# Single-core channel attention on Trainium2: K^T Q copied out of its PSUM banks, V cast moved to ScalarE, steps of one unit reordered

## The chip, the cores and the metric

The kernel runs on one core of a Trainium2 chip. The metric is device time in microseconds (us) of one execution. Engines are abbreviated as in the profile: PE is TensorE (PEld its weight loads), DVE is VectorE, ACT is ScalarE, POOL is GpSimd, SP starts the transfers. "Pitch" below is the time from the start of one unit's gram matmuls to the next unit's. TensorE is called "warm" when a gram takes about 1.07 us and "cold" when it takes about 1.90: in the kernel before, the granted clock was 1.00 at a gram of 1.07 us (at 161.74 us) and 0.50 at one of 1.90 us (at 81.00 us).

## The reference

For 8 x 12 heads with Q, K, V of 512 x 64 fp32:

```python
Q_norm = Q / (norm(Q, axis=-2) + 1e-10)          # columns of length 512 normalised
K_norm = K / (norm(K, axis=-2) + 1e-10)
attn = einsum('bhnd,bhne->bhde', Q_norm, K_norm)  # 64 x 64 per head
attn = softmax(attn, axis=-1)
return einsum('bhnd,bhde->bhne', V, attn)
```

## The kernel before

A unit is four heads; there are U = 24. Q and K of a unit are cast side by side into one bf16 tile `qkb`, and 64 small matmuls form its gram matrix: Q^T Q and K^T K give the norms (their diagonals), K^T Q the logits. The logits are K^T Q, scaled by 1/|k| (`kqs`), transposed by matmuls (`lgdup`), scaled by 1/|q| (`sl`), then exp, sum, normalise (`ab`). `ab` is doubled onto the other 64 partitions by a matmul. V is cast, transposed (`vps`, `vt`) and multiplied (`po`, `so`).

```python
def grams(u):
    g = gbuf[:, :, u % 2]                 # a tile in PSUM, two slots per head in use
    ...  nc.tensor.matmul(g[:, h], x, x, start=(t == 0), stop=(t == R - 1), ...)

def scale_k(u):                           # K^T Q times 1/|k|, read from the gram tile
    nc.vector.tensor_tensor(out=kk[D:], in0=gbuf[D:, :, u % 2, 0:D], in1=rq[u]..., op=ALU.mult)
...
for s in range(U + 3):                    # program order of one step
    on(load_qk, s + 3); on(load_v, s + 1); on(store, s - 6)
    on(casts, s + 1)                      # VectorE: Q and K
    on(scale_k, s - 1)                    # VectorE
    on(normalise, s - 2)                  # VectorE
    on(grams, s)                          # TensorE
    on(norms, s)                          # VectorE, then GpSimd for 1/norm
    on(vtrans, s - 2); on(outs, s - 3)    # TensorE, ScalarE copies
    on(logits, s - 1); on(scale_q, s - 1) # TensorE, VectorE
    on(cast_v, s - 1)                     # VectorE
    on(doubled, s - 2)                    # TensorE, ScalarE copy
    on(exps, s - 1)                       # ScalarE
```

In the trace each engine takes its instructions in this order (the steady unit in the prediction shows it). "Gram banks" below means the PSUM tile `gbuf`; the bank that logits and doubled attention share is the PSUM tile `lgdup`.

## Time and profile before

| | before |
|---|---|
| time, median of 3 runs | 180.92 us |
| profiled span | 177.2 us |
| gram of unit 3 / of unit 23 starts at | 24.97 / 161.74 us |
| pitch in the steady stretch | 6.83 us |

From the page of the kernel before: the busy time of each engine with its share of the span, then, over 40 slices of 4.4 us each, the TensorE clock in tenths and the bytes moved.

```profile
PE 104.3 (59%) x2712; PEld 84.9 (48%) x2712; DVE 110.2 (62%) x384; ACT 68.0 (38%) x121; POOL 29.0 (16%) x35
...
PEclk9999999686786786876876876867867867869995
...
GB/s 215 382 421 411 410 403 409 411 409 413 378 378 340 258 352 312 276 363 285 279 362 268 287 388 252 295 355 265 322 230 142 102 235 122 0 122 122 118 184 175
```

No engine is full, the clock is down to six to eight tenths from the eighth slice to near the end, and transfers slacken from about 410 to some 300 GB/s from the eleventh slice on: I read all three as engines waiting for each other. Which waits, the prediction shows.

### The profile page before, as it was taken

How to read it: one execution, taken by the hardware profiler on the slowest of the kernel's cores; microseconds unless marked ns; L12 is line 12 of the kernel's file. 1: busy time of each engine (PE TensorE's matmuls, PEld its weight loads, DVE VectorE, ACT ScalarE, POOL GpSimd, SP SyncE). 2: the span in 40 equal slices, each digit the busy share in tenths (PEclk: the TensorE clock that was granted, in tenths of full speed). 3: DMA queues.
4: the chain of work that ended last, by engine and by line, in shares of the span. 5: the costliest groups of instructions: out<-in, count | busy, mean ns of one | idle time of the engine just before them, and what ended most of it. 6: DMA issues, size and time to landing. Idle time of an engine off the chain costs nothing.

```text
span 177.2 us, 6265 instructions
## 1 busy us (share of the span) xinstructions
PE 104.3 (59%) x2712; PEld 84.9 (48%) x2712; DVE 110.2 (62%) x384; ACT 68.0 (38%) x121; POOL 29.0 (16%) x35
## 2 busy tenths in 40 slices
PE   0414847648559468477486485495594584677640
PEld 0314745537437346356365365274373473465430
DVE  0477585764765866857757757757758658567720
ACT  2000215154162361450541642632623614606981
POOL 5035202012022021120120220220220210201300
PEclk9999999686786786876876876867867867869995
DMA  5999999999999889898898898898865273033244
GB/s 215 382 421 411 410 403 409 411 409 413 378 378 340 258 352 312 276 363 285 279 362 268 287 388 252 295 355 265 322 230 142 102 235 122 0 122 122 118 184 175
DMA packets 13850, 50.72 MB, mean 286 GB/s; under 512 B 1536, under 2 KB 1536, under 8 KB 13824
## 3 DMA queue, kind: packets, MB, share of 16 engines
q1 hardware_dynamic: 13824, 50.34, 77.3%
q8 instruction: 21, 0.34, 0.8%
q14 instruction: 5, 0.04, 0.1%
HBM read 37.75 MB, written 12.58 MB: 284 GB/s over the span
## 4 chain that ended last, share of the span: by engine, by line
PE 51%; DVE 32%; DMA 4%; issue 3%; ACT 3%; POOL 2%; SPq 1%; ACTq 0%; POOLq 0%
PE gram L88 24%; PE vps L139 12%; PE lgdup L111 8%; PE po L151 8%; DVE vb L80 7%; DVE qkb L76 7%; DVE qkb L75 7%; DVE kqs L105 6%; DVE sl L115 5%; DMA kf<-in_K_dram 4%; POOL rq L100 2%; ACT so L155 2%; DVE scr L95 1%; ACT ab L133 1%; ACT ex L119 0%
## 5 line engine op out<-in xcount | busy, mean ns | idle before, releaser
L88 PE MATMUL gram<-qkb 32*128 32x128 bf16 x1536 | 44.4, 302 | 54.0 <-DVE kqs L105 47.9
L88 PEld LDWEIGHTS <-qkb 32*128 32x128 bf16 x1536 | 40.1, 137 | 69.4 <-issue 61.2
L141 ACT COPY vt<-vps 128x1024 bf16<-128x1024 bf16 x24 | 24.3, 1012 | 86.6 <-PE vps L139 86.4
L100 POOL TENSOR_TENSOR rq<-nsq,mhalf 128x4 f32<-128x4 f32 x24 | 26.6, 1107 | 136.0 <-DVE nsq L95 136.0
L95 DVE CUSTOM_DVE_ANT_0 scr<-gram,ident 128x128 f32<-128x128 f32 x96 | 22.2, 287 | 20.6 <-PE gram L88 20.6
L115 DVE TENSOR_TENSOR sl<-lgdup,rq 64x256 f32<-64x256 f32 x24 | 10.0, 417 | 28.0 <-PE lgdup L111 27.8
L155 ACT COPY so<-po 128x512 f32<-128x512 f32 x48 | 26.0, 598 | 0.5 <-PE po L151 0.5
L139 PE MATMUL vps<-identb,vb 128*128 128x128 bf16 x192 | 23.6, 298 | 0.7 <-DVE vb L80 0.7
L139 PEld LDWEIGHTS <-vb 128*128 128x128 bf16 x192 | 17.5, 134 | 6.7 <-issue 4.1
L75 DVE CAST qkb<-qf 128x1024 bf16<-128x1024 f32 x24 | 16.3, 680 | 5.5 <-DMA qf<-in_Q_dram 5.5
L151 PE MATMUL po<-ab,vt 128*32 128x128 bf16 x768 | 17.1, 239 | 1.1 <-ACT ab L133 1.1
L111 PE MATMUL lgdup<-ident,kqs 64*64 64x64 f32 x192 | 17.4, 235 | 0.0
L76 DVE CAST qkb<-kf 128x1024 bf16<-128x1024 f32 x24 | 16.3, 680 | 1.5 <-DMA kf<-in_K_dram 1.5
L80 DVE CAST vb<-vf 128x1024 bf16<-128x1024 f32 x24 | 16.2, 675 | 0.0
L151 PEld LDWEIGHTS <-vt 128*32 128x32 bf16 x768 | 12.9, 107 | 6.1 <-issue 5.0
L119 ACT ACTIVATE ex<-sl 64x256 f32<-64x256 f32 x24 | 10.0, 417 | 14.5 <-DVE sl L115 14.0
L111 PEld LDWEIGHTS lgdup<-ident,kqs 64*64 64x64 f32 x192 | 14.0, 144 | 2.9 <-issue 0.8
L132 PE MATMUL lgdup<-ab,identb 64*64 64x256 bf16 x24 | 6.6, 275 | 12.3 <-DVE sl L115 11.7
L123 DVE TENSOR_REDUCE esum<-ex 64x4 f32<-64x256 f32 x24 | 9.9, 411 | 1.8 <-ACT ex L119 1.2
L105 DVE TENSOR_TENSOR kqs<-gram,rq 64x256 f32<-64x256 f32 x24 | 10.3, 428 | 0.9
L127 DVE TENSOR_TENSOR ab<-ex,rinv 64x256 bf16<-64x256 f32 x24 | 10.0, 417 | 0.8
L133 ACT CAST ab<-lgdup 64x256 bf16<-64x256 f32 x24 | 8.8, 367 | 2.9 <-PE lgdup L132 2.3
(13 smaller groups left out, 18.5 us busy)
## 6 DMA issues: line engine op xcount, KB each, us to landing
qf<-in_Q_dram SPq DMA_DIRECT2D x24, 512.0 KB, 7.3
kf<-in_K_dram SPq DMA_DIRECT2D x24, 512.0 KB, 8.1
vf<-in_V_dram SPq DMA_DIRECT2D x24, 512.0 KB, 4.5
out_dram<-so SPq DMA_DIRECT2D x24, 512.0 KB, 5.0
```

What stands on the lines that cost most here:

```text
L75: nc.vector.tensor_copy(t_[:, :, 0:D], qf[u])
L76: nc.vector.tensor_copy(t_[:, :, D:], kf[u])
L80: nc.vector.tensor_copy(w.rearrange("p t d -> p (t d)"), vf[u])
L88: nc.tensor.matmul(g[:, h], x, x, start=(t == 0), stop=(t == R - 1), tile_position=(NV * h, 0))
L95: nc.vector.tensor_tensor_reduce(out=scr, in0=gbuf[:, h, u % 2], in1=ident, scale=1.0, scalar=1e-20, op0=ALU.mult, op1=ALU.add, accum_out= ...
L100: nc.gpsimd.tensor_tensor(out=r, in0=n2, in1=mhalf, op=ALU.pow)
L105: nc.vector.tensor_tensor(out=kk[D:], in0=gbuf[D:, :, u % 2, 0:D], in1=rq[u][D:, :, None].to_broadcast([D, HU, D]), op=ALU.mult,)
L111: nc.tensor.matmul(lg[:, h, :], kqs[u][D:, h, :], ident[D:, D:], tile_position=(D, 0))
L139: nc.tensor.transpose(ps[:, t, :], vb[u][:, t, :], identb)
L141: nc.scalar.copy(w, ps)
L151: nc.tensor.matmul(po[rows, k, :], vt[u][:, TP // 2 * i + k, rows], a[:, h].rearrange("p a d -> p (a d)"), tile_position=(0, NV * h),)
L155: nc.scalar.copy(s[:, TP // 2 * i:TP // 2 * (i + 1), :], po)
```

## The change

Its intent: take the reading of the gram banks off the slow path. ScalarE copies K^T Q out right behind the grams, unscaled, so that only that copy and the norms hold them; VectorE scales the copy later, from SBUF. The V cast goes to ScalarE, and exp, normalising and the doubling are moved to other places in the step. Cut to its core:

```diff
-    V_AHEAD = LOAD_AHEAD - 2
+    V_AHEAD = LOAD_AHEAD - 3
     def cast_v(u):
-        nc.vector.tensor_copy(w..., vf[u])
+        nc.scalar.copy(w..., vf[u])
+    def keep_kq(u):
+        nc.scalar.copy(kq[u][D:], gbuf[D:, :, 0:D])
     def scale_k(u):
-            in0=gbuf[D:, :, u % 2, 0:D], ...
+            in0=kq[u][D:], ...
@@ one step @@
+        on(exps, s - 2)
+        on(cast_v, s - 2)
+        on(cast_q, s + 1)
+        on(normalise, s - 2)
         on(scale_k, s - 1)
         on(grams, s)
+        on(keep_kq, s)
         on(norms, s)
+        on(cast_k, s + 1)
+        outs(s - 3, s - 2)     # output halves; doubling of s - 2 between the two copies
         on(logits, s - 1)
         on(scale_q, s - 1)
+        on(vtrans, s - 2)
```

The first V is also no longer loaded in front of the loop, and the gram buffer has one slot per head.

More of the change, by code (lines that the diff above doesn't have):

```diff
@@ L53 @@
     LOAD_AHEAD = 3
-    V_AHEAD = LOAD_AHEAD - 2
-    CAST_AHEAD = 1
+    V_AHEAD = LOAD_AHEAD - 3
     STORE_LAG = 6
-    qf, kf, vf, vb, qkb, nsq, rq, kqs, sl, ex, vt, so = ({} for _ in range(12))
+    qf, kf, vf, vb, qkb, nsq, rq, kqs, sl, ex, vt, so, kq = ({} for _ in range(13))
     def load_qk(u):
@@ L71, in store, with cast_q, cast_k @@
         nc.sync.dma_start(out=Of[u], in_=so[u].rearrange("p t d -> p (t d)"))
-    def casts(u):
-        t_ = qkb[u] = qkp.tile([128, R, 2 * D], BF16, name="qkb")
-        nc.vector.tensor_copy(t_[:, :, 0:D], qf[u])
-        nc.vector.tensor_copy(t_[:, :, D:], kf[u])
+    def cast_q(u):
+        qkb[u] = qkp.tile([128, R, 2 * D], BF16, name="qkb")
+        nc.vector.tensor_copy(qkb[u][:, :, 0:D], qf[u])
+    def cast_k(u):
+        nc.vector.tensor_copy(qkb[u][:, :, D:], kf[u])
     def cast_v(u):
         w = vb[u] = vbp.tile([128, TP, 2 * D], BF16, name="vb")
-        nc.vector.tensor_copy(w.rearrange("p t d -> p (t d)"), vf[u])
+        nc.scalar.copy(w.rearrange("p t d -> p (t d)"), vf[u])
     def grams(u):
-        g = gbuf[:, :, u % 2]
         for t in range(R):
@@ L87, in grams @@
                 x = qkb[u][NV * h:NV * (h + 1), t, :]
-                nc.tensor.matmul(g[:, h], x, x, start=(t == 0), stop=(t == R - 1), tile_position=(NV * h, 0))
+                nc.tensor.matmul(gbuf[:, h, 0:2 * D], x, x, start=(t == 0), stop=(t == R - 1), tile_position=(NV * h, 0))
+    def keep_kq(u):
+        kq[u] = small.tile([128, HU, D], F32, name="kq")
+        nc.scalar.copy(kq[u][D:], gbuf[D:, :, 0:D])
     def norms(u):
@@ L95, in norms @@
             nc.vector.tensor_tensor_reduce(
-                out=scr, in0=gbuf[:, h, u % 2], in1=ident, scale=1.0, scalar=1e-20,
+                out=scr, in0=gbuf[:, h, 0:2 * D], in1=ident, scale=1.0, scalar=1e-20,
                 op0=ALU.mult, op1=ALU.add, accum_out=n2[:, h:h + 1],
@@ L105, in scale_k @@
         nc.vector.tensor_tensor(
-            out=kk[D:], in0=gbuf[D:, :, u % 2, 0:D], in1=rq[u][D:, :, None].to_broadcast([D, HU, D]), op=ALU.mult,
+            out=kk[D:], in0=kq[u][D:], in1=rq[u][D:, :, None].to_broadcast([D, HU, D]), op=ALU.mult,
         )
@@ L127, in normalise @@
         nc.vector.tensor_tensor(out=a[0:D, :, 0, :], in0=ex[u], in1=ri[:, :, None].to_broadcast([D, HU, D]), op=ALU.mult)
-    def doubled(u):
-        a = abuf[u % len(abuf)]
-        nc.tensor.matmul(dup[D:], identb[0:D, 0:D], a[0:D, :, 0, :], tile_position=(0, D))
-        nc.scalar.copy(a[D:, :, 1, :], dup[D:])
     def vtrans(u):
@@ L141, in vtrans, with outs, half @@
         nc.scalar.copy(w, ps)
-    def outs(u):
-        s = so[u] = sop.tile([128, TP, 2 * D], F32, name="so")
-        a = abuf[u % len(abuf)]
-        for i in range(2):
+    def outs(u, u2):
+        def half(i):
             po = ps_o.tile([128, TP // 2, 2 * D], F32, name="po")
@@ L154, in outs, with keep @@
                     )
-            nc.scalar.copy(s[:, TP // 2 * i:TP // 2 * (i + 1), :], po)
-    gbuf = ps_g.tile([128, HU, 4, 2 * D], F32, name="gram")
+            return po
+        def keep(i, po):
+            nc.scalar.copy(so[u][:, TP // 2 * i:TP // 2 * (i + 1), :], po)
+        if 0 <= u < U:
+            a = abuf[u % len(abuf)]
+            so[u] = sop.tile([128, TP, 2 * D], F32, name="so")
+            p0 = half(0)
+            keep(0, p0)
+            p1 = half(1)
+        if 0 <= u2 < U:
+            a2 = abuf[u2 % len(abuf)]
+            nc.tensor.matmul(dup[D:], identb[0:D, 0:D], a2[0:D, :, 0, :], tile_position=(0, D))
+            nc.scalar.copy(a2[D:, :, 1, :], dup[D:])
+        if 0 <= u < U:
+            keep(1, p1)
+    gbuf = ps_g.tile([128, HU, 512], F32, name="gram")
     ltile = ps_l.tile([128, 2, HU, D], F32, name="lgdup")
@@ L164 @@
         load_qk(u)
-        if u - 2 >= 0:
-            load_v(u - 2)
     ident = const.tile([128, 128], F32, name="ident")
@@ L178 @@
         abuf.append(a)
-    for u in range(CAST_AHEAD):
-        casts(u)
     def on(f, u):
@@ L185, in on @@
             f(u)
+    on(cast_q, 0)
+    on(cast_k, 0)
     for s in range(U + 3):
@@ L190 @@
         on(store, s - STORE_LAG)
-        on(casts, s + CAST_AHEAD)
+        on(exps, s - 2)
+        on(cast_v, s - 2)
+        on(cast_q, s + 1)
+        on(normalise, s - 2)
         on(scale_k, s - 1)
-        on(normalise, s - 2)
         on(grams, s)
+        on(keep_kq, s)
         on(norms, s)
-        on(vtrans, s - 2)
-        on(outs, s - 3)
+        on(cast_k, s + 1)
+        outs(s - 3, s - 2)
         on(logits, s - 1)
         on(scale_q, s - 1)
-        on(cast_v, s - 1)
-        on(doubled, s - 2)
-        on(exps, s - 1)
+        on(vtrans, s - 2)
     for u in range(U + 3 - STORE_LAG, U):
```

## The prediction

> **What bounds the kernel now.** I read the page first, for which engine is full. None is: VectorE is busy 62%, TensorE 59%, ScalarE 38%. So waits decide, and the list of waits comes next. Its largest line on TensorE is this (columns: total us, times, longest):
>
> ```profile
> PE gram L88 <- DVE kqs L105: 47.9, 23, 4.6
> ...
> PE lgdup L132 <- DVE sl L115: 11.7, 23, 0.5
> ```
>
> The gram matmuls wait 47.9 us for `kqs`, the scaling of K^T Q of the unit before, though the two use different slots of the gram buffer. The doubling matmul L132 waits for `sl` although it writes other partitions of the same bank. [...] Then the timeline of one steady unit shows what stands in front of `kqs` (start, length, instruction):
>
> ```profile
> 81.00 1.90 PE L88 MATMUL gram<-qkb 32*128 32x128 bf16 x64 [2.00 <-DVE kqs L105]
> ...
> 82.83 1.03 PE L139 MATMUL vps<-identb,vb 128*128 128x128 bf16 x8
> ...
> 83.80 0.67 PE L151 MATMUL po<-ab,vt 128*32 128x128 bf16 x32
> ...
> 84.39 0.68 PE L111 MATMUL lgdup<-ident,kqs 64*64 64x64 f32 x8
> ...
> 85.11 0.42 DVE L115 TENSOR_TENSOR sl<-lgdup,rq 64x256 f32<-64x256 f32 x1 [1.22 <-PE lgdup L111]
> 85.45 0.68 DVE L80 CAST vb<-vf 128x1024 bf16<-128x1024 f32 x1
> 85.58 0.27 PE L132 MATMUL lgdup<-ab,identb 64*64 64x256 bf16 x1 [0.51 <-DVE sl L115]
> ...
> 86.05 0.68 DVE L75 CAST qkb<-qf 128x1024 bf16<-128x1024 f32 x1
> ...
> 86.65 0.68 DVE L76 CAST qkb<-kf 128x1024 bf16<-128x1024 f32 x1
> ...
> 87.36 0.43 DVE L105 TENSOR_TENSOR kqs<-gram,rq 64x256 f32<-64x256 f32 x1
> ...
> 87.84 1.90 PE L88 MATMUL gram<-qkb 32*128 32x128 bf16 x64 [2.00 <-DVE kqs L105]
> ```
>
> One closed loop, start to start: gram to `sl` 4.11 us (gram 1.90, transposes, outputs and logits on TensorE in program order, 85.11 - 81.00), `sl` 0.34, the V cast 0.60, the Q cast 0.60, the K cast 0.71, `kqs` 0.48, next gram. That is 6.84; the grams lie 6.84 apart here, and (161.74 - 6.08) / 23 = 6.77 apart over the whole run (gram starts of the timeline). Three casts stand inside this loop only because VectorE takes them ahead of `kqs`.
>
> TensorE's clock adds to it. At the end of the run the same matmuls are shorter:
>
> ```profile
> 161.74 1.07 PE L88 MATMUL gram<-qkb 32*128 32x128 bf16 x64 [0.79 <-DVE kqs L105]
> ...
> 162.74 0.62 PE L139 MATMUL vps<-identb,vb 128*128 128x128 bf16 x8
> ...
> 163.29 0.63 PE L151 MATMUL po<-ab,vt 128*32 128x128 bf16 x32
> ...
> 163.85 0.68 PE L111 MATMUL lgdup<-ident,kqs 64*64 64x64 f32 x8
> ```
>
> A warm gram is 1.07 us against 1.90, the transposes 0.62 against 1.03. The wait of 2.00 us before each gram makes it start cold in every steady unit.
>
> [...] the trace has 1.012 and 0.367 to 0.417, and two `so` copies of 0.598 in 1.08. [...] I use the trace's figure (last column GB/s):
>
> ```profile
> 38.00:44.00 6.00, 4.32 (x112) 3.68 (x112) 3.49 (x15) 1.95 (x4) 1.01 (x1) 0.72 1.03 416
> ```
>
> **The change part by part.** Costs come from these rows (the last before the bar is the mean ns):
>
> ```profile
> L141 ACT COPY vt<-vps 128x1024 bf16<-128x1024 bf16 x24 | 24.3, 1012 | 86.6 <-PE vps L139 86.4
> ...
> L155 ACT COPY so<-po 128x512 f32<-128x512 f32 x48 | 26.0, 598 | 0.5 <-PE po L151 0.5
> ...
> L119 ACT ACTIVATE ex<-sl 64x256 f32<-64x256 f32 x24 | 10.0, 417 | 14.5 <-DVE sl L115 14.0
> ...
> L133 ACT CAST ab<-lgdup 64x256 bf16<-64x256 f32 x24 | 8.8, 367 | 2.9 <-PE lgdup L132 2.3
> ```
>
> VectorE loses the V cast, 24 x 0.675 = 16.2 us. ScalarE gains it as a copy of 1024 elements a partition, 24 x 1.02, and `keep_kq`, shaped like L133, 24 x 0.37: 33.4 us, from 68.0 to about 101. TensorE does the same work. `kqs` now reads SBUF and no longer holds the grams. A gram waits instead for the norms and `keep_kq` of the unit before, which follow that gram directly, and for its K cast behind them. This removes the old loop: none of sl, casts, kqs lies between logits and the next gram.
>
> The new loop I find by walking each queue in program order. Time 0 is the end of the transposes of one step.
> ScalarE: `vt` copy 0.13 to 1.14; exp from 1.05 to 1.47 (neighbours overlap); V cast 1.40 to 2.42; `keep_kq` 2.33 to 2.70; first `so` copy 2.62 to 3.2; copy of the doubled attention 3.12 to 3.49.
> TensorE: gram 0.1 to 2.0 if cold, 1.2 if warm; both output halves by 2.7; doubling at 2.6 to 2.85. Then logits, which share the bank with the doubled copy and so start at 3.55: 0.65 warm, 1.1 cold. Then transposes, a 0.1 us step and 0.6 warm, 1.0 cold: the next time 0 falls at 4.95 warm, 5.75 cold.
> VectorE: after exp, reduce, reciprocal and `ab` (start to start 0.45 + 0.20 + 0.42) until 2.5; `kqs` 2.93; norms after `keep_kq`, 2.97 to 3.9; K cast 4.5, so the next gram could start at 4.6, which is not last; `sl` to 4.95, Q cast to 5.5 beside the next gram. GpSimd's `rq` (1.0 us after the norms) is done long before its reader in the next step.
> So the bound becomes **a ScalarE to TensorE round trip** of 5 to 5.7 us; I take the middle, 5.35.
>
> The floor below it: a unit moves 4 x 512 KB = 2.10 MB, at 410 GB/s 5.1 us. It lies just under the loop.
>
> The sum. Start: K of unit 0 is there at 5.3, gram 0 at 6.1; unit 1 waits for its K (8.7), norms and cast: 10.0; unit 2 13.9; unit 3 follows the first V, whose load now stands behind four Q/K pairs and lands near 15 (each load 1.28 us at 410 GB/s), cast, `keep_kq`, norms, cast, doubling, logits, transposes: gram 3 at 18.4, against 24.97 now. Steady: 20 units x 5.35 = 107, gram 23 at 125.4 (now 161.74). Tail: step 23 5.2; step 24 without grams 4.7; step 25 3.9 with its `vt` copy behind the others, then outputs and last copies, 2.5; store 4.0 (now from 173.2 to 177.2): 20.3, against 15.5 now, because ScalarE has more to do there. Span 145.7; the runs' median lies 180.92 - 177.2 = 3.7 above the profiled span, so **149.5 us**.
>
> **Rivals.** (a) *Transfers bind.* The DMA share was already 0.90 at 313 GB/s in the steady stretch, which speaks for it; 412 and 416 GB/s in the early windows against. If steady traffic reached only 365, a unit takes 5.75: about 157. At 410 it is a floor of 5.1: 144. (b) *The clock decides.* Always warm, 4.95, but transfers then hold it at 5.1: 144.5. Always cold, 5.75: about 157.5. The old unit locked to two clock windows; locked again it would stay 6.83 and gain only the start, some 174 to 180. Against it: even the cold loop needs only 5.75. (c) *ScalarE full.* Its busy sum a unit would be 1.01 + 0.42 + 1.02 + 0.37 + 1.20 + 0.37 = 4.4 us, 80% of 5.35. In-order waits inside that queue, say `keep_kq` held by a late gram with everything behind it, could add 0.5 us a unit: about 160. (d) *V cast late, norms late*: if the norms had to wait for `keep_kq` and the cast behind them ended after the transposes, the gram would wait. My slack there is 0.4 us, the thinnest in the walk; half a microsecond more costs at most 0.1 to 0.3 a unit, 2 to 6 us.
>
> **Range and chances.** The clock gives 144 to 158, transfers raise the low side, unforeseen waits only the high side: 141 to 163. All of 20 units would have to lose 1.3 us against my loop to come within 2% of 180.9. Faster 0.94, same 0.04, slower 0.02.
>
> **What would show it.** Right: grams about 5.3 us apart; TensorE's wait for `kqs` gone, replaced by one of logits L111 for the doubled copy on ScalarE; the norms released by `keep_kq`; ScalarE at two thirds of the span or more; V cast near 1.02 us; DMA near 400 GB/s until the loads end; gram 3 near 18. Wrong: grams waiting for the K cast or for norms (d), ScalarE waiting long on a gram (c), casts waiting on loads in the middle of the run (a), or a pitch of 6.83 again (b).

Gram 3 at 18.4, 107 for 20 units, 20.3 for the tail and 3.7 for the offset make about 149.5 us.

- Order: the gram waits 47.9 us for `kqs` of another slot, the doubling 11.7 us for `sl` on other partitions. So using another slot or other partitions of a tile did not remove the wait; that the ordering goes by bank is not shown.
- Clock: in the trace of the kernel before, the granted clock is full for 3.41 us and half for 3.41 us in turn from 29 to 159 us, and 6.83 us is two of these steps. They are the "clock windows". In the kernel after, its stretches last 3.41, 6.83, 10.24 or 13.65 us, one to four steps, up to the last one. That the wait of 2.00 us is what makes the gram cold, and that the unit was locked to two steps, were inferences; experiments 3 and 4 test them.
- ScalarE: the `vt` copy of 1024 elements a partition took 1.012 us, instructions of 256 elements 0.367 to 0.417. Neighbours overlap by 0.10 us (`vt` and `so` copy) and by 0.11 to 0.12 us (two `so` copies). The 1.02 us of the V cast is an estimate near the first of these; 1.032 was measured after.
- Transfers: 410 GB/s in the mean from 20 to 45 us of the kernel before, loads and stores together. The floor of 5.1 us is an estimate from it.

## The result, and the profile after

| | before | after |
|---|---|---|
| time, median | 180.85 us (4 runs) | 154.96 us (4 runs, 152.59 to 155.51) |
| ratio of the fast runs | | 0.849, 95% interval 0.840 to 0.859 |
| gram of unit 3 / of unit 23 starts at | 24.97 / 161.74 us | 20.56 / 132.31 us |
| mean pitch, unit 3 to 23 | 6.84 us | 5.59 us |
| from the last gram's start to the end | 15.5 us | 21.4 us |

A ratio is the mean time of one kernel's fast runs over that of the other's fast runs of the same rounds, so not quite the ratio of the medians. Two of the four runs after, the profiled one among them, are labelled slow: on one core this only means more than 1.5% above the fastest run of the same kernel. Their mean clock is 0.77; the two fast runs have 0.79 and 0.77. The span of the profiled run, 153.7 us, is therefore on the long side (the fast ones: 150.8 and 152.7). The pitches above are from this profile.

The same page lines, of the kernel after:

```profile
PE 106.8 (69%) x2712; PEld 85.8 (56%) x2712; DVE 95.5 (62%) x360; ACT 101.0 (66%) x169; POOL 43.8 (29%) x35
...
PEclk9999999995569776895985589596855599585555
...
GB/s 190 321 402 417 410 408 406 403 414 407 417 411 413 416 410 417 410 415 417 408 419 411 418 419 410 421 413 378 390 320 189 270 4 136 141 82 59 136 136 136
```

ScalarE went from 68.0 to 101.0 us busy, VectorE from 110.2 to 95.5. The transfers now stay above 400 GB/s for 25 slices instead of 8. TensorE's clock falls to half in many slices.

The list of waits after (total us, times, longest):

```profile
PE lgdup L116 <- ACT ab L168: 19.8, 23, 1.9
...
PE gram L88 <- DVE qkb L77: 9.4, 3, 6.0
...
PE po L150 <- issue: 3.7, 5, 1.3
```

The wait of 47.9 us for `kqs` is gone. What is new in its place is the logits' wait of 19.8 us for the doubled attention on ScalarE (`ab` L168): both use the tile `lgdup`. The grams wait for the K cast three times only. The output matmuls waited 3.7 us for nothing that the profile shows ("issue"), which the kernel before never did; the experiments come back to this.

One steady unit of the timeline (start, length, instruction):

```profile
87.36 1.89 PE L88 MATMUL gram<-qkb 32*128 32x128 bf16 x64
87.52 1.01 ACT L140 COPY vt<-vps 128x1024 bf16<-128x1024 bf16 x1 [1.61 <-PE vps L138]
...
88.42 0.41 ACT L124 ACTIVATE ex<-sl 64x256 f32<-64x256 f32 x1
88.74 1.03 ACT L81 CAST vb<-vf 128x1024 bf16<-128x1024 f32 x1
...
89.80 0.37 ACT L93 COPY kq<-gram 64x256 f32<-64x256 f32 x1
...
90.19 0.59 ACT L157 COPY so<-po 128x512 f32<-128x512 f32 x1
90.42 0.29 DVE L100 CUSTOM_DVE_ANT_0 scr<-gram,ident 128x128 f32<-128x128 f32 x1
...
90.80 0.37 ACT L168 CAST ab<-lgdup 64x256 bf16<-64x256 f32 x1
...
91.22 0.68 PE L116 MATMUL lgdup<-ident,kqs 64*64 64x64 f32 x8 [0.96 <-ACT ab L168]
...
91.83 0.62 PE L138 MATMUL vps<-identb,vb 128*128 128x128 bf16 x8
...
92.38 1.07 PE L88 MATMUL gram<-qkb 32*128 32x128 bf16 x64
```

This is the predicted round trip. Read it from the first gram: the `vt` copy starts as the transposes before it end, then ScalarE goes through exp, V cast, `keep_kq`, one `so` copy and the doubled copy without a pause (87.52 to 91.17); the logits start 0.05 us later, then the transposes, then the next gram at 92.38. Nothing on VectorE stands in it: the norms follow at 90.42, and the K cast behind them ends at 91.96, before the next gram.

### The profile page after: what moved, and what is told of

It reads as the page before. It is cut to its first block, busy times and chain, and to the rows that moved or that the text cites. A ratio compares the mean times of both kernels' runs of the same rounds, so it can differ in the third digit from the quotient of the medians.

```text
span 153.7 us, 6358 instructions
## 1 busy us (share of the span) xinstructions
PE 106.8 (69%) x2712; PEld 85.8 (56%) x2712; DVE 95.5 (62%) x360; ACT 101.0 (66%) x169; POOL 43.8 (29%) x35
## 4 chain that ended last, share of the span: by engine, by line
PE 38%; ACT 33%; issue 14%; DMA 8%; SPq 2%; DVE 1%; ACTq 1%
PE lgdup L116 14%; PE vps L138 12%; ACT vb L81 8%; DMA vf<-in_V_dram 8%; ACT so L157 8%; PE gram L88 7%; ACT ab L168 6%; ACT kq L93 5%; PE po L150 4%; ACT ex L124 4%; ACT vt L140 3%; SPq L63 1%; SPq L62 1%; PE lgdup L167 1%; DVE ab L132 1%
## 5 line engine op out<-in xcount | busy, mean ns | idle before, releaser
L105 POOL TENSOR_TENSOR rq<-nsq,mhalf 128x4 f32<-128x4 f32 x24 | 41.4, 1725 | 93.0 <-DVE nsq L100 93.0
L88 PE MATMUL gram<-qkb 32*128 32x128 bf16 x1536 | 40.1, 282 | 9.4 <-DVE qkb L77 9.4
L88 PEld LDWEIGHTS <-qkb 32*128 32x128 bf16 x1536 | 34.6, 127 | 13.3 <-DVE qkb L77 9.8
L116 PE MATMUL lgdup<-ident,kqs 64*64 64x64 f32 x192 | 22.0, 276 | 19.8 <-ACT ab L168 19.8
L116 PEld LDWEIGHTS lgdup<-ident,kqs 64*64 64x64 f32 x192 | 17.9, 179 | 30.1 <-ACT ab L168 29.9
L81 ACT CAST vb<-vf 128x1024 bf16<-128x1024 f32 x24 | 24.8, 1032 | 1.8 <-DMA vf<-in_V_dram 1.8
L150 PE MATMUL po<-ab,vt 128*32 128x128 bf16 x768 | 20.4, 259 | 7.9 <-ACT vt L140 4.1
L138 PE MATMUL vps<-identb,vb 128*128 128x128 bf16 x192 | 21.5, 280 | 0.0
L93 ACT COPY kq<-gram 64x256 f32<-64x256 f32 x24 | 8.8, 367 | 10.4 <-PE gram L88 9.8
L110 DVE TENSOR_TENSOR kqs<-kq,rq 64x256 f32<-64x256 f32 x24 | 10.1, 423 | 0.8
```

Source lines behind the costliest of these rows:

```text
L81: nc.scalar.copy(w.rearrange("p t d -> p (t d)"), vf[u])
L88: nc.tensor.matmul(gbuf[:, h, 0:2 * D], x, x, start=(t == 0), stop=(t == R - 1), tile_position=(NV * h, 0))
L93: nc.scalar.copy(kq[u][D:], gbuf[D:, :, 0:D])
L105: nc.gpsimd.tensor_tensor(out=r, in0=n2, in1=mhalf, op=ALU.pow)
L116: nc.tensor.matmul(lg[:, h, :], kqs[u][D:, h, :], ident[D:, D:], tile_position=(D, 0))
L138: nc.tensor.transpose(ps[:, t, :], vb[u][:, t, :], identb)
```

## The experiments

All ratios are against the kernel before, in the same rounds; that kernel ran at 179.0 to 180.9 us in the different batches, so ratios are compared here, not medians. Three kernels give wrong results on purpose, and are marked so. In the batch of experiments 4, 7, 8 and 10 two of the four runs of the kernel before are labelled slow, and the record calls these four verdicts unclear; their intervals rest on the fast runs that are left.

### 1. The copy alone

The kernel before, plus the copy and nothing else:

```diff
+    def keep_kq(u):
+        nc.scalar.copy(kq[u][D:], gbuf[D:, :, u % 2, 0:D])
-            in0=gbuf[D:, :, u % 2, 0:D], ...   # scale_k
+            in0=kq[u][D:], ...
         on(grams, s)
+        on(keep_kq, s)
```

> The kernel before with one part of the change: K^T Q is copied out unscaled by ScalarE right behind the grams and scaled later from SBUF; everything else stays (V cast on VectorE, old order). Theory (the old loop was closed only by the scaling that read the gram banks): the gram's wait for kqs is gone, the pitch falls from 6.83 us to the next bound, VectorE's own sum of about 4.8 us or the cold TensorE chain of 5.8, so about 5.2, and the time falls to about 146 (143 to 158), most of the gain or all of it. Rival (the moved V cast and the spread softmax carry a good part of the gain): above 165.

Measured: correct, 146.75 us, ratio 0.818 (0.810 to 0.825). It beats the full change, whose interval starts at 0.840. In its timeline the next gram starts while VectorE is still at the V cast:

```profile
89.82 0.68 DVE L80 CAST vb<-vf 128x1024 bf16<-128x1024 f32 x1
89.95 0.27 PE L136 MATMUL lgdup<-ab,identb 64*64 64x256 bf16 x1 [0.51 <-DVE sl L119]
...
90.14 1.07 PE L88 MATMUL gram<-qkb 32*128 32x128 bf16 x64
```

Against the fence of the prediction, sl, V cast and doubling stand in the same places, but the gram no longer waits for Q cast, K cast and `kqs`. Mean pitch 5.37 us. What ends last in most units is now a loop that none of the accounts had: norms on VectorE, `rq` (1/norm) on GpSimd, then `kqs` and normalising on VectorE, then the next norms. `kqs` starts within 0.04 us of the end of `rq` in 21 of 24 units. `rq` takes 1.01 us in the steady units of the kernel before, but 2.37 in the mean here and up to 2.97. Over all the runs its length goes with the VectorE casts that run beside it: 1.01 us with none, 1.1 to 1.7 with one, 1.3 to 2.2 with two, 2.0 to 3.1 with three. Experiment 11 shows this loop almost undisturbed.

Set against the profile of the full change (153.7 - 143.9 = 9.8 us of span): start 20.56 - 19.52 = 1.0, twenty pitches 4.4, and the end 21.4 - 17.0 = 4.4 us. So everything else in the change lost part of what the copy won: 9.8 of 33.3 us between these profiles, of which the changed kernel's is a long one; by the ratios of fast runs 3 of 18 points, a sixth.

### 2. The rest of the change without the copy

The changed kernel, with `kqs` again scaled straight from the gram banks:

```diff
-            in0=kq[u][D:], ...
+            in0=gbuf[D:, :, 0:D], ...
-        on(keep_kq, s)
```

> The changed kernel without the copy: K^T Q is scaled straight out of the gram banks, as before, but in the new order of steps and with the V cast on ScalarE. Theory (the copy alone makes the gain, since it takes the scaling out of the wait in front of the gram): the gram waits for kqs again, which now stands behind exp and the normalising steps; the walk gives 6.7 us warm to 8.2 cold a unit, time 175 to 205, no better than the kernel before. Rival (order and V cast carry a part of their own): well below 175.

Measured: correct, 219.05 us, ratio 1.222 (1.217 to 1.227): worse than the kernel before by more than I expected. Its list of waits:

```profile
PE gram L88 <- DVE kqs L110: 69.9, 23, 3.3
```

The gram waits up to 3.3 us again, now for a `kqs` that stands behind the `vt` copy, exp and normalising; every gram is cold at 1.89 to 1.90, and pitches from unit 4 on are 7.97 to 8.84 us, where my walk had at most 8.2. Direction right, size short. With experiment 1: the copy carries the whole gain, and the new order is bearable only with it.

### 3. The V cast alone

```diff
     def cast_v(u):                      # in the kernel before
-        nc.vector.tensor_copy(...)
+        nc.scalar.copy(...)
```

> The kernel before with only the V cast moved to ScalarE. Theory (the cast stood in the loop in front of kqs): the loop is 0.60 us shorter, 6.84 to 6.24, about 14 us less, 166. Rival (the unit is locked to two clock windows of 3.41 us): pitch stays 6.83, time within 2% of 181.

Measured: correct, 179.07 us, ratio 0.999 (0.992 to 1.007). My theory failed and the rival holds. 16 us of VectorE work left the loop, 0.60 us a unit, and nothing came of it. The wait in front of the gram did fall, from 2.00 to 1.30 or 1.40, but TensorE's work became slower by as much: 118.1 us busy instead of 104.3, mean clock 0.65 instead of 0.80. From unit 3 to unit 7 the pitch is 6.3 to 6.5, near the 6.24 of the theory, and gram 7 starts 3.9 us earlier than in the kernel before. Then pitches repeat 6.22, 7.05, 7.04, 6.99: four units in 27.30 us. The granted clock in the two traces changes in steps of 3.41 us: in the kernel before it is full for 3.41 us and half for 3.41 us in turn from 29 to 159 us, so that its 6.83 us are two steps; here it is full for 3.41 and half for 23.89 in turn from 61 us on, and 27.30 us are eight. One gram in four is warm (those at 90.96, 118.27 and 145.57 us took 1.07 us, those between 1.89 to 1.90). I read this as a pitch that the clock holds in these units, not the sum of the work; experiment 4 tests it. The 4.1 us that gram 23 is ahead are mostly given back at the end, which is cold (gram 23 took 1.89 us instead of 1.07): 19.1 us from the last gram's start instead of 15.5.

### 4. The same lock, broken by work that nobody needs

The kernel before, with four extra matmuls of 512 columns, whose result is never read, in the gap in front of each gram:

```diff
+    def warm(u):
+        x = ps_v.tile([128, 512], F32, name="vps")
+        for i in range(4):
+            nc.tensor.matmul(x, identb, qkb[u][:, 4 * i % R:4 * i % R + 4, :]...)
         on(doubled, s - 2)
+        on(warm, s)
```

> The kernel before with four extra matmuls of 512 columns, read by nobody, in TensorE's 2.0 us gap in front of each gram. Theory (that gap lets the clock fall, and the unit is locked to two clock windows): gram 1.90 to 1.07, transposes 1.03 to 0.62, the loop 6.84 to 5.6, time about 153, faster although work was added. Rival (the clock does not follow activity in this gap, or the extra work delays the gram): 180 or more.

Measured: correct, 161.62 us, ratio 0.896 (0.867 to 0.925), 10% faster with work added; its slowest run, 164.37, is far below the fastest of the kernel before in this batch, 177.21. The extra matmuls and the gram behind them in its TensorE timeline:

```profile
80.70 1.04 PE L138 MATMUL vps<-qkb,identb 128*128 128x512 bf16 x4
82.81 1.07 PE L88 MATMUL gram<-qkb 32*128 32x128 bf16 x64 [1.07 <-DVE kqs L105]
```

The extra matmuls (1.04 us) fill half of the gap, the gram is warm, and the pitch is 5.61, the 5.6 of the expectation. It is not always so: the next gram after this one was cold again, a few pitches are near 7, the mean from unit 2 on is 5.81, and the time is almost 9 us above the expected 153. With the gap half filled the mean granted clock was 0.94, against 0.80 in the kernel before: the half clock was a cost of TensorE's idling there, 0.83 us on the gram and 0.41 us on the transposes, 1.24 us a unit on top of the wait.

### 5. The V cast back on VectorE in the changed kernel

```diff
-        nc.scalar.copy(w..., vf[u])
+        nc.vector.tensor_copy(w..., vf[u])
```

> The changed kernel with the V cast back on VectorE. Theory (the new bound is the round trip ScalarE to TensorE, in which the V cast stands with 0.93 us): the walk gives 4.7 us warm and 5.5 cold, pitch 5.2 to 5.4 with transfers as a floor near 5.1, time about 149, faster than the changed kernel's 155. Rival (VectorE bound again, as its share was in the kernel before): slower than 155, to 160 or more. Rival (transfers bound): 155 unchanged.

Measured: correct, 151.92 us, ratio 0.848 (0.841 to 0.854): the same as the full change at 0.849. The walk was right on the pitch where nothing else happened (4.66 to 4.89, warm), but two pitches in the steady stretch were 7.29 and 8.06: in the second one TensorE stood for 3.0 us in the middle of its output matmuls, waiting for nothing that the profile shows. Neither my expectation nor the rivals had this. Such stops add up to 7.9 us here.

### 6. The transposes in front of the logits

```diff
+        on(vtrans, s - 2)
         on(logits, s - 1)
         on(scale_q, s - 1)
-        on(vtrans, s - 2)
```

> The changed kernel with one swap: the V transposes stand before the logits in TensorE's order, in the gap in which TensorE waits for the doubled copy. Theory (round trip bound): logits and transposes no longer both lie between the doubled copy and the next vt copy; the walk gives about 4.6 us, so the floor of the transfers, about 5.1, takes over: pitch 5.1, time about 146. Rival (transfers at 415 GB/s already bound the changed kernel): 153 to 155, unchanged. Rival (cold clock sets TensorE's own sum): TensorE's cold sum is 5.5, so about 153.

Measured: correct, 147.14 us, ratio 0.819 (0.812 to 0.826), against 0.849. One swap brings 3 points, so the round trip did bound the changed kernel: the transposes now run while ScalarE makes the doubled copy. Warm pitches are 4.13 to 4.73. But here, too, TensorE stops without a reason; a stretch of its timeline:

```profile
28.16 0.67 PE L88 MATMUL gram<-qkb 32*128 32x128 bf16 x34 [0.15 <-DVE qkb L77]
29.97 0.89 PE L88 MATMUL gram<-qkb 32*128 32x128 bf16 x30 [1.14 <-issue]
...
33.90 0.89 PE L88 MATMUL gram<-qkb 32*128 32x128 bf16 x49
36.27 0.40 PE L88 MATMUL gram<-qkb 32*128 32x128 bf16 x15 [1.47 <-issue]
...
38.75 1.07 PE L88 MATMUL gram<-qkb 32*128 32x128 bf16 x63
42.19 0.21 PE L88 MATMUL gram<-qkb 32*128 32x128 bf16 x1 [2.38 <-issue]
```

Three grams in a row are cut: after 34 of their 64 matmuls, after 49, after 63. A unit has 113 matmuls and as many weight loads on TensorE (2712 / 24 each), so from one stop to the next are 2 x (113 + 15) = 256 and 2 x (113 + 14) = 254 instructions.

### 7 and 8. Fewer transfers (wrong results on purpose)

V is loaded for the first five units only and used again, in the changed kernel and in that of experiment 6:

```diff
     def load_v(u):
+        if u >= 5:
+            vf[u] = vf[u % 5]
+            return
```

> The changed kernel with V loaded for five units only and used again (wrong result on purpose): a quarter of the traffic goes. Theory (round trip of ScalarE and TensorE bounds, transfers are a floor just below it): pitch stays between 5.0 warm and 5.85 cold, about 5.5, time 151 to 155. Rival (transfers at 415 GB/s bound): loads and stores fall to 1.57 MB a unit, 3.8 us; pitch and time fall clearly, below 147. A third account (TensorE stalls a few times for 1 to 3 us on its own instruction stream because the transfers saturate): those stalls, 3.7 us at the output matmuls in the changed kernel, shrink, 2 to 4 us in all.

Measured: 149.84 us, ratio 0.838 (0.822 to 0.853), overlapping the 0.849 of the changed kernel; its stalls (3.2 + 0.8 us) did not shrink. The pitches are still mostly 4.97 to 5.05 warm and 5.83 to 5.88 cold. So V's bytes are not what sets these pitches; whether the few us are real is not settled.

> The transposes-first kernel (147.1 us) with V loaded for five units only (wrong result on purpose). Its TensorE stood 18.5 us in all in front of gram and output matmuls with nothing to wait for. If the saturated transfers hold up the instruction stream, these stalls fall below 5 us and the time to about 135 (pitch 4.5 warm to 5.2 cold). If the cold clock and the engines' own work set the pitch, the time stays at 144 to 147.

Measured: 138.19 us, ratio 0.773 (0.755 to 0.792), from 0.819. The stalls only fell from 18.9 to 12.3 us; the transfers were still near 410 GB/s for the first half. Between my two expectations, and undecided; hence the next run.

### 9. Hardly any loads (wrong results on purpose)

Experiment 8, with Q and K treated like V:

```diff
     def load_qk(u):
+        if u >= 5:
+            qf[u], kf[u] = qf[u % 5], kf[u % 5]
+            return
```

> The transposes-first kernel with only the first five units of Q, K and V loaded (wrong result on purpose), so that hardly more than the stores remain. If saturated transfers cause TensorE's stalls in front of gram and output matmuls that wait for nothing (18.5 us in all; 12.3 without V), they fall below 4 us and the time to about 130. If they stay at 10 us or more, the transfers are not their cause.

Measured: 123.68 us, ratio 0.690 (0.686 to 0.693). Waits for "issue" of TensorE, first experiment 6, then this run:

```profile
PE gram L88 <- issue: 10.9, 8, 2.4
...
PE po L150 <- issue: 7.6, 4, 2.7
```

```profile
PE gram L94 <- issue: 0.3, 1, 0.3
```

The stalls are gone, every gram from unit 6 on is warm or nearly so (clock 0.94), and the pitch is 4.16 us over and over. The loads, with which the transfers ran at 412 GB/s (30 to 46 us of experiment 6), therefore cost the transposes-first kernel about 23 us, its colder clock (0.78 against 0.94) included, and past the first units no wait in its list names a load. A line of the page of experiment 6, from its list of DMA queues (packets, MB, share of the 16 engines), points at how:

```profile
q8 instruction: 21, 0.34, 1.0%
```

21 packets of 0.34 MB are 16 KB each, and TensorE's 2 x 2712 instructions divided by 21 are 258, the distance between two stops. So the stops look like waits for the next block of TensorE's own program. The DMA records of the traces fit that: the three stops shown above end at 29.97, 36.27 and 42.19 us, and packets of this queue had landed at 28.67, 34.79 and 40.90. All 13 stops of experiment 6, and 82 of the 85 in all runs, end 1.2 to 1.6 us after such a packet has landed, though the packets lie about 6 us apart; in the changed kernel all five do, by 1.25 to 1.44 us. A packet itself takes 1.06 us in the mean both in experiment 6 and here; how the loads delay it before it starts, these traces do not show.

### 10. Two extra matmuls in the changed kernel

As in experiment 4, two instead of four, behind the doubling, where TensorE waits for the doubled copy:

```diff
         outs(s - 3, s - 2)
+        on(warm, s)
```

> The changed kernel with two extra matmuls of 512 columns, read by nobody, in the gap in which TensorE waits for the doubled copy. Theory (two thirds of its units run with a cold clock and take 5.85 instead of 5.02): nearly all units warm, pitch 5.0 to 5.2, time 144 to 148. Rival (transfers bound, or the clock falls all the same): 153 to 157.

Measured: correct, 151.97 us, ratio 0.850 (0.834 to 0.866), the same as without. The clock did rise, from 0.77 to 0.86, and many pitches are 4.97 to 5.12; but the stalls grew from 3.7 to 12.8 us. What the higher clock won, the stops took.

### 11. Two extra matmuls with the copy alone

Experiment 1, with two of them between the logits and the doubling:

```diff
         on(logits, s - 1)
+        on(warm, s)
```

> The kernel before with the copy alone (146.8 us), plus two extra matmuls of 512 columns, read by nobody, between the logits and the doubling, where TensorE waits 0.5 to 1.0 us. Theory (its pitch of 5.37 is a mix of 4.6 warm and 5.5 to 5.7 cold): mostly warm, pitch about 5.0, time about 140 and the best of all. Rival (its pitch is set by transfers or by TensorE waiting for its own instructions): 145 to 149.

Measured: correct, 146.93 us, ratio 0.822 (0.815 to 0.828), the same as experiment 1 with 0.818, although the clock rose from 0.76 to 0.90. The time is the one that the rival named, but not for its reasons: 12 of the 20 pitches from unit 3 on lie between 5.38 and 5.41 us, and what holds them is the loop through GpSimd of experiment 1:

```profile
51.59 2.86 POOL L104 TENSOR_TENSOR rq<-nsq,mhalf 128x4 f32<-128x4 f32 x1 [2.54 <-DVE nsq L99]
...
54.49 0.42 DVE L109 TENSOR_TENSOR kqs<-kq,rq 64x256 f32<-64x256 f32 x1 [0.90 <-POOL rq L104]
```

VectorE waits for `rq` (14.4 us in all, 16 times), scales K^T Q at 54.49, normalises, takes the next norms from 55.94 on, and the next `rq` starts at 57.00, 5.41 us after this one. TensorE's stops on "issue" are 13.8 us here (7.6 in experiment 1), but one of 1.55 us at 53.88 lies inside a pitch of 5.40 and does not lengthen it.

### 12. Transposes first, and V loaded one place earlier

Experiment 6, with the first V loaded behind the third Q/K pair and each later V one step earlier, as in the kernel before:

```diff
-    V_AHEAD = LOAD_AHEAD - 3
+    V_AHEAD = LOAD_AHEAD - 2
     for u in range(LOAD_AHEAD):
         load_qk(u)
+        if u == 2:
+            load_v(0)
```

> The transposes-first kernel with the first V loaded one place earlier, as in the kernel before. Theory (the first V cast stood waiting 1.8 us for its load behind four Q/K pairs): gram 3 comes 1 to 2 us sooner and the time falls by as much, to 145 to 146. Rival (the start is hidden by later waits): no change from 147.

Measured: correct, 145.48 us, ratio 0.811 (0.804 to 0.818). Gram 3 starts at 18.31 instead of 19.18 us, a little less than the 1 to 2 us expected. It is the fastest correct kernel by its median, but its interval overlaps those of experiments 1 and 6, so that the time falls is not shown.

## Why the prediction was right or wrong

The time, 149.5 us with a range of 141 to 163, held: 154.96.

**The old loop.** Right. The ordering between `kqs` and the gram was the closing link: with that link cut and nothing else, the kernel takes 18% less time (experiment 1). But the sentence that the three casts stand in the loop, and so cost it their length, was incomplete: taking one of them out brought nothing (experiment 3), and the mean granted clock fell from 0.80 to 0.65. I had noted that 6.83 us is two steps of the clock and did not draw this conclusion for the parts of the change. The step in front of a drop to half clock was not an idle one: from 83.92 to 87.33 us of the kernel before, TensorE was busy for 1.42 us, and the clock fell to half at 87.33.

**The norms held by the copy.** Assumed in the walk and named as a sign, and seen only at the start: the list of waits has the norms held by `keep_kq` twice, 2.5 us in all, both in the first units. In the steady unit shown VectorE is still at `kqs` (89.97 to 90.39) when `keep_kq` ends at 90.17.

**The new loop.** Right in its links (the steady unit above) and nearly in its ends: 4.95 warm (the terms of the walk add up to 4.90) and 5.75 cold were forecast, 5.02 and mostly 5.82 to 5.88 measured. Experiment 6, which shortens just this chain, gained 3 points.

**The mean of the loop.** This is the term that was mis-sized. I took the middle of warm and cold, 5.35; 13 of the 20 pitches were cold ones (5.66 us or more), and the mean is 5.59. About half of the difference is the share of cold pitches, half that both kinds are a tenth of a microsecond longer than forecast (5.06 and 5.87 in the mean, TensorE's stops included). Twenty times 0.24 is 4.8 us. With steady gaps of no more than about 1 us at a time (0.96 in the unit shown) the mean granted clock of this run was still 0.77.

**Start, end, offset.** Gram 3 was forecast at 18.4 and came at 20.56: the first V was there at 16.8, not 15, and everything behind it was cold (logits 1.11 us, transposes 1.04, gram 3 1.89). The end took 21.4 instead of 20.3, again cold (granted clock 0.50 from 137.35 us on). The profiled run lay only 1.8 us above its span, not 3.7: I had set the median of other runs against the span of a profiled run that itself took 179.29, 2.1 above its span. That error ran the other way and hid 1.9 us of the rest by luck. Sum: 149.5 + 4.8 + 2.2 + 1.1 - 1.9 = 155.7, against 155.51 of that run.

**Rival (a), transfers.** I called them a floor at 5.1 us that would show as casts waiting for loads. No cast waits in the middle of any run. The loads showed themselves in TensorE's own stops (18.9 us in experiment 6, 0.3 us with the loads gone in experiment 9), which I had not thought of. In the changed kernel they are small (3.7 us).

**Rival (b), the clock.** It decided, but between the two ends that I gave, not at one of them; no new pitch of 6.83 appeared (mean 5.59).

**Rivals (c) and (d).** ScalarE waited for a gram twice, before the first two copies, 9.8 us in all; the gram waited for the K cast only at the start. Neither cost anything in the steady stretch.

**What the prediction missed** is how the gain divides. It treated the moved V cast and the new order as neutral. Together they give back a sixth of what the copy wins: ratios 0.849 against 0.818. Which of the moved steps costs how much is only partly shown: the V cast alone makes no difference that can be measured (experiment 5), the place of the transposes makes 3 points (experiment 6), and the end of the run, where three units drain one after the other through the longer chain, about 4 of the 10 us of span.

## What to carry to other kernels

Before counting what an engine saves, find the one link that closes the loop, and cut it alone first: here a 0.37 us copy out of the shared gram tile was worth 32 us, and the rest of the change took some of it back. Then look for the link that closes the next loop, on engines that look idle too: with the copy alone it ran through GpSimd, 41% busy. Compare a steady pitch with the steps of the granted clock in the trace: here, at 6.83 us and steps of 3.41, taking 0.60 us a unit out of the loop brought nothing (ratio 0.999, experiment 3), and filling half of the 2.00 us gap with useless matmuls gave 0.896 (experiment 4); where something else held the time, such matmuls gained nothing (0.850 against 0.849 in experiment 10, 0.822 against 0.818 in 11). And with transfers near 410 GB/s, look for an engine that stops with nothing to wait for: here such stops came to 18.9 us in one kernel, and they fit waits of TensorE for its own instructions.
